# Paired rests transposed into the fourth turned tile's PSUM bank, with an earlier low-rank load and three reorderings in a hybrid attention block

## The chip, the cores and the metric

The kernel runs on one core of a Trainium2 chip. The metric is the device time of one execution in microseconds (us). Five engines take part: TensorE (PE: matmuls and transposes, and PEld, its weight loads), VectorE (DVE), ScalarE (ACT), GpSimd (POOL), and the queues that issue transfers, SyncE (SP) above all. Each engine works through its own instructions in order and waits on semaphores for the others. PE writes only into PSUM, which has eight banks of 128 partitions by 512 float32 values here, and DVE and ACT read the results from there.

## The reference

One encoder layer with two token mixers that read the same normalised input of 512 tokens by 2048 features.

```python
h = rms_norm(x) * (1 + scale) + shift
proj = h @ w_in                       # 2048 -> 7200 columns
aq, ak, av, ag, gq, gk, gv, gg, lr_f, lr_b = split(proj)

# 16 heads x 64, three dilated windows, merged by their softmax denominators
outs, lses = zip(*[dilated_window_attention(aq, ak, av, rel_bias, w, d)
                   for w, d in ((128, 1), (512, 4), (2048, 16))])
att = sum(softmax(lses)[p] * outs[p] for p in range(3))
a_out = att * silu(ag)

# 4 heads, dk 128, dv 256, forward and backward scan
log_g = log_sigmoid(lr @ gate_up + gate_bias) / 16
g_out = rms_norm(gla(q, k, v, log_g_f) + flip(gla(flip(...)))) * gain * silu(gg)

y = concat([a_out, g_out]) @ w_out
out = rms_norm(x + gate * y) * final_gain
```

## The kernel before

**Tiling.** Every large product is done in three matmuls (`three`, L228 to L232): high part by high part, high by low, low by high, with the operands split into two float32r halves. One such matmul is 128 x 128 weights by 512 columns. A *unit* is a 2048 x 512 block of projection columns: `unit` (L1159) runs over 8 groups of weights, 4 output tiles and 2 inner steps, 64 ticks of three matmuls each, and puts the list of side work that it is given between the ticks. Each item of that list has a place between 0 and 1, the share of the 64 ticks after which it is recorded; items at the same place keep the list's order, and items at 1 or more spill into the next unit. PE's order is the order of recording. The orders of DVE, ACT, POOL and SP come from a scheduler that sees the recorded dependences and priorities.

**The order of units.** Start (`sta`, `stb`), then `qk2`, `qk4`, `qk6`, `gk`, each with the attention of four heads beside it (some 200 to 444 us of the span), then the values of the linear attention (`values_unit`, with `gla_head(0)` beside it), `ag0`, `ag1`, `gg0` (each with one more `gla_head`), `gg1`, and the output products `P1`, `P7`, `P6`, `P4`, `P5`, `P3`, `P2` for two pairs of column blocks.

**PSUM.** Two rings: `pj` with five banks (`PJ`), four of which hold a unit's outputs, and `pa` with three (`PA`), through which the side work goes. 

**One head of attention.** A head has four query tiles. `score` (L829) makes a tile's logits (two matmuls into a `pa` bank), DVE adds the bias and takes the minimum (L847), ACT takes the exponent (L851), DVE the reciprocal (L854), POOL scales (L864). The last columns of tiles 1 to 3 are scaled into free columns of tile 0, so that four small *rests* share one 128 x 128 block. Two items later `turn` (L868) transposes three 128 x 128 blocks of the tile on PE (L882) into a `pa` bank `t`; ACT copies them into the high operand `pth` (L888) and DVE takes the low operand `ptl` (L889). When the fourth tile is turned (`i == 3`), `rest` (L896) first transposes the block of rests (L899) into a `pj` bank of its own, `r`, and its four quarters of 32 x 128 are copied and split: for the first two quarters ACT (L906, twice), then DVE (L908, twice), then the same for the other two. `values` (L910) is the head's product with the values (L915, L917), which reads `pth` and `ptl`. The heads below are counted from 0 to 15.

**The low-rank weights.** After unit `gk`, 256 KB of weights are loaded into `lrb` (L1303, SP) and split into `lrs` by ACT (L1306) and DVE (L1307); `low_rank` (L1310) uses them within the values.

**A head of linear attention.** `gla_head` (L1012) returns ten steps: `gates` of the two directions, `turn` of the two (PE transposes `kt`, L1062, ACT copies `kit`, L1064), `states` of the two (PE `kv`, L1074; DVE L1081 and L1086; POOL L1084; ACT L1091), `att` (L1101), two `outs` (L1123), `norm`. `GLA_FIRST` holds the places of head 0 and `GLA_AT` those of the others.

**Before the output products.** `to_s1(1)` and `to_s2(1)` (L1471, L1474: DVE, 128 x 1024 each) form sums for the products `P6` and `P5`. They stand behind the eviction of `gg1` (L1202). A step given to `later(pair, product, group, go)` is recorded when that group's weights are split.

Of the kernel before, what the change touches and what calls it, by code (L numbers as in the profile page):

```python
# [18 lines left out]
P = 128  # L19
S = 512  # L20
D = 2048
KT = D // P
# [95 lines left out]
REST_OF = (14, 11, 2, 15)  # L118
TOKENS = [slice(256 * c + a, 256 * c + 256, 2) for a in range(2) for c in range(2)]

GLA_AT = (0.01, 0.02, 0.33, 0.46, 0.46, 0.56, 0.64, 0.76, 0.76, 0.88)
GLA_FIRST = (0.3, 0.38, 0.55, 0.62, 0.775, 0.81, 0.86, 0.9, 0.92, 0.97)

SUMS_IN = {"ag0": 8, "ag1": 8, "gg0": 8}

# [66 lines left out]
def block_kernel(ctx: ExitStack, tc: tile.TileContext, a: dict):  # L192
# [15 lines left out]
    def T2(name, dt=F32, parts=P):  # L208
        return t2.tile([parts, 512], dt, tag="t2", name=name)
# [4 lines left out]
    def PJ(name):  # L214
        return pp.tile([P, 512], F32, tag="pj", bufs=5, name=name)

    def PA(name):
        return pp.tile([P, 512], F32, tag="pa", bufs=3, name=name)
# [599 lines left out]
    def attention(pairs):  # L818
# [49 lines left out]
        def turn(h, i):  # L868
            def go():
                if not pts:  # L870
                    for z in "hl":
                        pts.append(B8(f"pt{z}", [16, P], F32R))
                        for at, to in ((2, 3), (11, 12)) + ((14, 16),) * (z == "h"):
                            nc.gpsimd.memset(pts[-1][:, at:to, :].bitcast(F32), 0.0)
                if i == 3:
                    rest(h)
                t = pr_.pop((h, i)) if i else pr_[h, i]
                pk = PA(f"t{h}{i}")
                first_ = 0 if i % 2 else 128
                for n_, (c, _) in enumerate(FULL[i]):  # L880
                    kt = (c - i - 1) % 4
                    nc.tensor.transpose(pk[:, n_ * P:n_ * P + P], t[:, first_ + kt * P:first_ + kt * P + P], ident)  # L882
                at, step = FULL[i][0][1], FULL[i][1][1] - FULL[i][0][1]
                hi, lo = (pt[:, at:at + 2 * step + 1:step, :] for pt in pts)
                src = pk[:, :3 * P].rearrange("p (k q) -> p k q", k=3)

                def parts():
                    act(hi, src, AF.Copy)  # L888
                    tt(lo, src, hi.bitcast(F32), op=ALU.subtract)  # L889
                if i or h == heads[0]:  # L890
                    parts()
                else:
                    held_parts.append(parts)
            return go

        def rest(h):  # L896

            pk = PJ(f"r{h}")
            nc.tensor.transpose(pk[:, :P], pr_.pop((h, 0))[:, 0:128], ident)  # L899
            hi, lo = pts  # L900
            to = [(hi, 0, hi, 32), (hi, 0, lo, 0), (hi, 96, lo, 96), (hi, 64, hi, 96)]
            parts = [(t[a:a + 32, REST_OF[i], :], u[b:b + 32, REST_OF[i], :], pk[96 - 32 * i:128 - 32 * i, :P])
                     for i, (t, a, u, b) in enumerate(to)]
            for pair in (parts[:2], parts[2:]):
                for up, _, of in pair:
                    act(up, of, AF.Copy)  # L906
                for up, low_, of in pair:
                    tt(low_, of, up.bitcast(F32), op=ALU.subtract)  # L908
# [103 lines left out]
    def gla_head(h):  # L1012
# [4 lines left out]
        def gates(d):  # L1017
            def go():
                n = f"{h}{d}"
                bias = gbias[:, 4 * d + h:4 * d + h + 1]  # L1020
                pz = PA("z" + n)
                mm(pz, gla["up"][:, d, h * P:h * P + P], gla["lr"], start=True, stop=True)
                e = T2("e" + n)
                act(e, pz, AF.Abs, bias=bias)
                act(e, e, AF.Exp, scale=-1.0)
                act(e, e, AF.Ln, bias=1.0)
                g = T2("g" + n)
                nc.vector.tensor_scalar(g, pz, bias, 0.0, op0=ALU.add, op1=ALU.min)  # L1028
# [12 lines left out]
                act(sc[:, 0, :], b3[:, :, im], AF.Exp, scale=1.0 / 16)  # L1041
                act(sc[:, 1, :], b3[:, :, il], AF.Exp, scale=1.0 / 16)
                bm = T2("bm" + n)
                bm3 = bm.rearrange("p (n t) -> p n t", n=4)
                tt(bm3, b3, b3[:, :, im:im + 1].to_broadcast([P, 4, P]), op=ALU.subtract)
                act(sc[:, 2, :], bm3[:, :, il], AF.Exp, scale=1.0 / 16)
                qi = T2("qi" + n)
                ki = T2("ki" + n)
                act(ki, bm, AF.Exp, scale=-1.0 / 16)
                act(qi, bm, AF.Exp, scale=1.0 / 16)  # L1050
                gq, gk = gla["q"][:, h, :], gla["k"][:, h, :]
                tt(ki, ki, gk, op=ALU.mult)
                tt(qi, qi, gq, op=ALU.mult)
                dirs[d].update(qi=qi, ki=ki, sc=sc, order=[0, 1, 2] if d == 0 else [3, 2, 1])
            return go

        def turn(d):
            def go():
                n, x = f"{h}{d}", dirs[d]
                pk = PA("kt" + n)  # L1060
                for j, c in enumerate(x["order"]):
                    nc.tensor.transpose(pk[:, j * P:j * P + P], x["ki"][:, c * P:c * P + P], ident)  # L1062
                x["kit"] = T2("kit" + n)
                act(x["kit"][:, :384], pk[:, :384], AF.Copy)  # L1064
            return go
# [65 lines left out]
        def norm():  # L1131
# [10 lines left out]
            for v in range(2):  # L1142
                m = 2 * h + v
                if m % 4 == 0:
# [2 lines left out]
                    op0=ALU.mult, op1=ALU.mult)  # L1147

        at = GLA_AT if h else GLA_FIRST
        return list(zip(at, [gates(0), gates(1), turn(0), turn(1), states(0), states(1), att,  # L1150
                             outs(0), outs(1), norm]))

    def urgent(go):
# [137 lines left out]
        for q in range(2):  # L1291
            qk_evict(p + 2 + q, ps[2 * q], ps[2 * q + 1])

    ps = unit("gk", False, attention((6, 7)))
    kp_.close()
    gs = mid.enter_context(tc.tile_pool(name="gs", bufs=1, reuse_waits="tile"))
    gla["k"] = B8("gkt", [4, 512])
# [1 line left out]
        act(gla["k"][:, i, :], ps[i], AF.Copy)  # L1299


    lrb = T2("lrb")
    nc.sync.dma_start(lrb.rearrange("p (k c) -> p k c", k=KT), a["w_lr"][0])  # L1303
    lrs = gp.tile([P, KT, 2, 32], F32R, tag="g", name="lrs")
    lrb3 = lrb.rearrange("p (k c) -> p k c", k=KT)
    act(lrs[:, :, 0, :], lrb3, AF.Copy)  # L1306
    tt(lrs[:, :, 1, :], lrb3, lrs[:, :, 0, :].bitcast(F32), op=ALU.subtract)  # L1307
    plr = PA("plr")
# [172 lines left out]
            (0.65, lambda: to_s1(0)), (0.8, lambda: to_s2(0))]  # L1481
    ps = unit("gg1", False, side + some_sums("gg1"))
    gate_evict(ps, cat[3], "g1")
    to_s1(1)
    to_s2(1)
    mid.close()
    op = ctx.enter_context(tc.tile_pool(name="op", bufs=1, reuse_waits="tile"))
    for e in "hl":
# [184 lines left out]
    for z in range(2):  # L1673
        later(0, "P4", 1 + 2 * z, lambda z=z: halves("A12", z, part(2 + z, 0))())
    later(0, "P1", 1, gate_row)
    later(0, "P4", 2, gain_rows(0))
    later(0, "P4", 3, x_again(0))
    later(1, "P7", 0, x_again(1))
# [129 lines left out]
```

## Time and profile before

| | before |
|---|---|
| time, median of 3 runs | 905.07 us (904.97 to 905.77) |
| profiled execution: time / span | 907.22 us / 905.4 us |
| granted TensorE clock, mean | 0.996 |
| PE busy | 890.0 us, 98% |
| DVE busy | 731.2 us, 81% |
| ACT busy | 491.6 us, 54% |
| POOL busy | 125.9 us, 14% |
| stretch of the attention, 200 to 444 us: PE / DVE / ACT busy | 241.78 / 210.54 / 146.46 of 244 us |

The span runs from the first to the last instruction of the profiled execution, whose own time is 1.8 us longer. Busy times are sums over an engine's instructions; those of different engines overlap. PE's matmuls are pipelined, so that a steady stream starts one every 0.23 us although each is shown as some 0.39 us long; a wait of PE is seen best as a step between two starts that is longer than that.

### The profile page before, as it was taken

The page shows a single profiled execution, that of the slowest core. Times are in us where ns is not written, and L with a number is a line of the kernel's source. Part 1 is how long each engine was busy: PE and PEld are TensorE (multiplying, and loading weights), DVE is VectorE, ACT ScalarE, POOL GpSimd, SP SyncE. Part 2 cuts the span into 40 slices and gives each one's busy share as a digit, 9 for nine tenths or more (in the row PEclk, how much of TensorE's full clock was granted, in tenths as well). Part 3 has the DMA queues.
Part 4 walks back from the last instruction along what each step waited for, and adds up shares of the span by engine and source line. Part 5 has one row for each costly group of instructions (what it writes and reads, how often), then busy time and mean ns, then how long its engine had stood idle before and what let it go on. Part 6 is the DMA issues. An engine that isn't in the chain of part 4 may idle for free.

```text
span 905.4 us, 12339 instructions
## 1 busy us (share of the span) xinstructions
PE 890.0 (98%) x4159; PEld 739.2 (82%) x4159; DVE 731.2 (81%) x1220; ACT 491.6 (54%) x841; POOL 125.9 (14%) x219
## 2 busy tenths in 40 slices
PE   8999999999999999999999999999999999999996
PEld 6888788888888888887778888888888888888885
DVE  7998799878989989888568668595787559797687
ACT  5554533466655745655657554373664248455454
POOL 0000000023323333243000101112020100000001
PEclk9999999999999999999999999999999999999999
DMA  9999489398798898998778879778796988777863
GB/s 342 401 411 363 186 344 367 134 306 226 202 266 273 247 265 247 249 298 223 232 260 255 311 206 308 206 249 262 231 279 208 275 286 289 282 288 249 289 238 154
DMA packets 65547, 242.33 MB, mean 268 GB/s; under 512 B 9190, under 2 KB 11526, under 8 KB 55883
## 3 DMA queue, kind: packets, MB, share of 16 engines
q1 hardware_dynamic: 58724, 199.23, 61.5%
q0 software_dynamic: 6464, 42.01, 19.4%
q8 instruction: 33, 0.54, 0.2%
q10 hardware_dynamic: 296, 0.30, 0.1%
q14 instruction: 30, 0.25, 0.1%
HBM read 224.64 MB, written 51.47 MB: 305 GB/s over the span
## 4 chain that ended last, share of the span: by engine, by line
PE 91%; DVE 3%; ACT 2%; DMA 2%; issue 1%; SPq 0%; DVEq 0%; ACTq 0%
PE ps_qk L230 5%; PE ps_qk L232 5%; PE ps_qk L231 5%; PE g L232 4%; PE g L230 4%; PE g L231 4%; PE stb L232 3%; PE stb L231 3%; PE stb L230 3%; PE ps_ag L232 3%; PE ps_ag L230 3%; PE ps_ag L231 3%; PE o L915 3%; PE sta L230 3%; PE sta L231 3%; PE sta L232 3%
## 5 line engine op out<-in xcount | busy, mean ns | idle before, releaser
L864 POOL TENSOR_SCALAR p<-p,st 128x32 f32<-128x32 f32 (+2 forms) x108 | 59.8, 565 | 159.9 <-DVE st L854 91.2
L328 DVE CUSTOM_DVE_ANT_0 cb<-cb,sb,c_bcond 128x2048 f32<-128x2048 f32 (+1 forms) x32 | 73.4, 2295 | 1.9 <-DMA cb<-in_wm 1.6
L851 ACT ACTIVATE p<-p,st 128x416 f32<-128x416 f32 x64 | 41.0, 641 | 49.2 <-DVE st L847 42.3
L429 POOL DMA_DIRECT2D T<-in_w_o x32 | 23.2, 725 | 159.4 <-ACT V2h L493 14.8
L888 ACT ACTIVATE pth<-t 128x384 fp32r<-128x384 f32 x64 | 31.0, 485 | 19.8 <-PE t L882 11.1
L889 DVE TENSOR_TENSOR ptl<-t,pth 128x384 fp32r<-128x384 f32 x64 | 35.2, 551 | 5.2 <-ACT pth L888 3.7
L882 PE MATMUL t<-c_ident,p 128*128 128x128 f32 x192 | 31.3, 272 | 0.0
L882 PEld LDWEIGHTS t<-c_ident,p 128*128 128x128 f32 x192 | 24.3, 139 | 7.9
L847 DVE CUSTOM_DVE_ANT_0 p<-s,g,st 128x256 f32<-128x256 f32 x64 | 27.7, 432 | 1.8
L847 DVE CUSTOM_DVE_ANT_0 p<-s,g 128x160 f32<-128x160 f32 x64 | 23.5, 367 | 4.2 <-PE s L840 3.5
L328 DVE CUSTOM_DVE_ANT_0 rawg<-rawg,crow,gate 128x1024 f32<-128x1024 f32 x16 | 20.4, 1279 | 4.0 <-DMA rawg<-in_wg 4.0
L1581 POOL TENSOR_SCALAR x<-x,rn 128x512 f32<-128x512 f32 x2 | 2.3, 1167 | 148.5 <-ACT rn L1570 148.5
L429 POOL DMA_DIRECT2D T3V<-in_w_gv x8 | 5.5, 687 | 125.1 <-ACT qk21h L493 118.7
L839 PE MATMUL s<-ks,qh 128*128 128x416 f32 x64 | 22.6, 353 | 0.0
L906 ACT ACTIVATE pth<-r 32x128 fp32r<-32x128 f32 x64 | 17.2, 269 | 9.9 <-PE r L899 4.5
L840 PE MATMUL s<-ks,ql 128*128 128x416 f32 x64 | 22.4, 350 | 0.0
L1091 ACT ACTIVATE sq<-st,sc 128x256 f32<-128x256 f32 x24 | 12.2, 506 | 18.6 <-DVE st L1081 10.0
L328 DVE CUSTOM_DVE_ANT_0 rawg<-rawg,crow,c_bcond 128x1024 f32<-128x1024 f32 x16 | 20.3, 1279 | 0.5 <-DVE g L1028 0.5
L429 POOL DMA_DIRECT2D T<-T x16 | 9.1, 571 | 79.9 <-ACT V8h L493 12.9
L915 PE MATMUL o<-pth,vv 128*128 128x512 f32 (+1 forms) x64 | 15.9, 369 | 2.2 <-DVE pth L908 1.1
L466 DVE TENSOR_TENSOR raw_O<-raw_O,raw_P 128x1024 f32<-128x1024 f32 x8 | 9.8, 1225 | 10.1 <-DMA raw_O<-in_w_o 7.8
L568 ACT ACTIVATE h_hi<-xt,shift 128x512 fp32r<-128x512 f32 x16 | 11.5, 721 | 10.3 <-DVE shift L328 9.5
(1661 smaller groups left out, 3151.6 us busy)
## 6 DMA issues: line engine op xcount, KB each, us to landing
cb<-in_wm SPq DMA_DIRECT2D x31, 1024.0 KB, 9.3
T<-in_w_o POOLq DMA_DIRECT2D x32, 512.0 KB, 6.5
rawg<-in_wg SPq DMA_DIRECT2D x32, 512.0 KB, 5.4
raw_O<-in_w_o SPq DMA_DIRECT2D x32, 512.0 KB, 4.6
raw_qk<-in_w_qk SPq DMA_DIRECT2D x24, 512.0 KB, 4.9
raw_O<-T SPq DMA_DIRECT2D x24, 512.0 KB, 5.0
rawb<-in_w_sb SPq DMA_DIRECT2D x16, 512.0 KB, 8.9
rawv<-in_wv SPq DMA_DIRECT2D x16, 512.0 KB, 5.6
```

Of the source, the lines that this page charges most:

```text
L230: mm(ps, lh, rh, start=first, stop=False, skip_group_check=more)
L231: mm(ps, ll, rh, start=False, stop=False, skip_group_check=more)
L232: mm(ps, lh, rl, start=False, stop=last, skip_group_check=more)
L328: return nc.vector.tensor_tensor_reduce(out=w, in0=w, in1=with_, op0=ALU.mult, op1=ALU.add, scale=1.0, scalar=init, accum_out=dst)
L429: move = nc.gpsimd.dma_start(dst, src, max_dma_last_dim=8192, **how).ins
L847: top = nc.vector.tensor_tensor_reduce(out=t[:, lo:hi], in0=ps[:, lo:hi], in1=gt[h][:, at:at + 2 * (hi - lo) - 1:2], op0=ALU.add, op1=ALU.min,
L851: act(t, t, AF.Exp, bias=st[:, 0:1], scale=-1.0, accum_out=st[:, 1:2])
L864: last["pool"] = nc.gpsimd.tensor_scalar(to, of, st[:, 2:3], 1.0, op0=ALU.mult, op1=ALU.mult).ins
L882: nc.tensor.transpose(pk[:, n_ * P:n_ * P + P], t[:, first_ + kt * P:first_ + kt * P + P], ident)
L888: act(hi, src, AF.Copy)
L889: tt(lo, src, hi.bitcast(F32), op=ALU.subtract)
L915: mm(po[:, P * a0:P * a1], vv[h // 4][:, c, h % 4, :], pt[:, at:at + (a1 - a0 - 1) * step + 1:step, :], start=n_ == z == 0, stop=False, sk ...
```

## The change

The rests' transpose no longer takes a bank of its own. `turn` takes its `pa` bank `t` first and hands `rest` the last quarter of it, columns 384 to 511; the three transposes of the fourth tile, which are recorded behind `rest`, write columns 0 to 383 of the same bank. Line numbers behind L892 fall by one or rise by a few. The load of `lrb` becomes an item at 0.7 of unit `gk`. In the linear attention the first direction's states come ahead of the second direction's turn for heads 1 to 3 (with the second turn at 0.47 in place of 0.46); for head 0 the places are swapped with the list, so that only its two `outs` move, from 0.9 and 0.92 to 0.91 and 0.93. `to_s1(1)` and `to_s2(1)` are recorded in group 1 of the first `P1`.

```diff
-GLA_AT = (0.01, 0.02, 0.33, 0.46, 0.46, 0.56, 0.64, 0.76, 0.76, 0.88)
-GLA_FIRST = (0.3, 0.38, 0.55, 0.62, 0.775, 0.81, 0.86, 0.9, 0.92, 0.97)
+GLA_AT = (0.01, 0.02, 0.33, 0.46, 0.47, 0.56, 0.64, 0.76, 0.76, 0.88)
+GLA_FIRST = (0.3, 0.38, 0.55, 0.775, 0.62, 0.81, 0.86, 0.91, 0.93, 0.97)
...
+                pk = PA(f"t{h}{i}")
                 if i == 3:
-                    rest(h)
+                    rest(h, pk[:, 3 * P:])
                 t = pr_.pop((h, i)) if i else pr_[h, i]
-                pk = PA(f"t{h}{i}")
...
-        def rest(h):
-
-            pk = PJ(f"r{h}")
-            nc.tensor.transpose(pk[:, :P], pr_.pop((h, 0))[:, 0:128], ident)
+        def rest(h, pk):
+
+            nc.tensor.transpose(pk, pr_.pop((h, 0))[:, 0:128], ident)
             hi, lo = pts
             to = [(hi, 0, hi, 32), (hi, 0, lo, 0), (hi, 96, lo, 96), (hi, 64, hi, 96)]
-            parts = [(t[a:a + 32, REST_OF[i], :], u[b:b + 32, REST_OF[i], :], pk[96 - 32 * i:128 - 32 * i, :P])
+            parts = [(t[a:a + 32, REST_OF[i], :], u[b:b + 32, REST_OF[i], :], pk[96 - 32 * i:128 - 32 * i, :])
                      for i, (t, a, u, b) in enumerate(to)]
...
-        return list(zip(at, [gates(0), gates(1), turn(0), turn(1), states(0), states(1), att,
+        return list(zip(at, [gates(0), gates(1), turn(0), states(0), turn(1), states(1), att,
                              outs(0), outs(1), norm]))
...
-    ps = unit("gk", False, attention((6, 7)))
+    lrb = []
+
+    def lr_load():
+        lrb.append(T2("lrb"))
+        nc.sync.dma_start(lrb[0].rearrange("p (k c) -> p k c", k=KT), a["w_lr"][0])
+
+    ps = unit("gk", False, attention((6, 7)) + [(0.7, lr_load)])
...
-    lrb = T2("lrb")
-    nc.sync.dma_start(lrb.rearrange("p (k c) -> p k c", k=KT), a["w_lr"][0])
...
-    to_s1(1)
-    to_s2(1)
...
+    later(0, "P1", 1, lambda: (to_s1(1), to_s2(1)))
```

The first place is PE where head 4's rests and fourth tile are transposed, in unit `qk4` (`ps_qk` its outputs, `p` the scaled tiles, `c_ident` the identity; in brackets the engines whose semaphores an instruction waits for). Before:

```order
L232 MATMUL ps_qk_0_2253<-h_lo,qk43h 128x512
L899 MATMUL r_2487<-c_ident,p_2324 128x128 [waits Pool_49]
L882 MATMUL t_2497<-c_ident,p_2409 128x128 [waits DVE_49,PE_49,Activation_49]
L882 MATMUL t_2497<-c_ident,p_2409 128x128 x2
L230 MATMUL ps_qk_1_2254<-h_hi,qk43h 128x512
L231 MATMUL ps_qk_1_2254<-h_hi,qk43l 128x512
L232 MATMUL ps_qk_1_2254<-h_lo,qk43h 128x512
```

The same place on PE after the change:

```order
L232 MATMUL ps_qk_0_2249<-h_lo,qk43h 128x512
L898 MATMUL t_2483<-c_ident,p_2320 128x128 [waits DVE_49,PE_49,Pool_49]
L882 MATMUL t_2483<-c_ident,p_2405 128x128 [waits DVE_49,Activation_49]
L882 MATMUL t_2483<-c_ident,p_2405 128x128 x2
L230 MATMUL ps_qk_1_2250<-h_hi,qk43h 128x512
L231 MATMUL ps_qk_1_2250<-h_hi,qk43l 128x512
L232 MATMUL ps_qk_1_2250<-h_lo,qk43h 128x512
```

All four transposes now write one tile, `t_2483`. The first of the three has a wait for DVE of its own, and in the built program the value that this wait asks for is the one that the fourth and last of head 4's L907 brings; this holds for each of the 16 heads. Before, head 4's wait for DVE asked for the L847 that had last read the bank.

The second place is DVE at the same head, where the low parts of the rests are taken (L908 before, L907 after; `rawv` is a bias sum beside the attention, `s` the next tile's logits). Before:

```order
L998 ISA rawv_2329,vbias_1498<-rawv_2329,shb 128x1024 [waits DMAHW6_49,DMAHW4_49]
L998 ISA vbias_1498 128x1
L854 RECIPROCAL st_2467<-st_2467 128x1 [waits Activation_49]
L908 TENSOR_TENSOR pth<-r_2487,pth 32x128 [waits PE_49]
L908 TENSOR_TENSOR ptl<-r_2487,pth 32x128
L847 ISA p_2509,st_2510<-s_2506,g_2341 128x160 [waits PE_49,Pool_49]
L847 ISA st_2510 128x1
L889 TENSOR_TENSOR ptl<-t_2497,pth 128x3x128
L847 ISA p_2509,st_2510<-s_2506,g_2341,st_2510 128x256 [waits DVE_49]
L847 ISA st_2510 128x1
L908 TENSOR_TENSOR ptl<-r_2487,pth 32x128 [waits Activation_49]
L1249 TENSOR_TENSOR S_2514<-S_2414,h_hi 128x512 [waits Pool_49]
```

The same place on DVE after the change:

```order
L997 ISA rawv_2325,vbias_1498<-rawv_2325,shb 128x1024 [waits DMAHW6_49,DMAHW4_49]
L997 ISA vbias_1498 128x1
L854 RECIPROCAL st_2463<-st_2463 128x1 [waits Activation_49]
L907 TENSOR_TENSOR pth<-t_2483,pth 32x128 [waits PE_49]
L907 TENSOR_TENSOR ptl<-t_2483,pth 32x128
L907 TENSOR_TENSOR ptl<-t_2483,pth 32x128 [waits Activation_49]
L907 TENSOR_TENSOR pth<-t_2483,pth 32x128
L889 TENSOR_TENSOR ptl<-t_2483,pth 128x3x128 [waits Activation_49]
L847 ISA p_2504,st_2505<-s_2501,g_2337 128x160 [waits PE_49,Pool_49]
```

The four low parts now stand together, ahead of the fourth tile's own low part (L889) and of the next logits; between the second and the third DVE waits for ACT. What stands ahead of the first is as it was.

The third place is PE in unit `gg0`, where head 3 of the linear attention turns its keys for the second direction (`kt`) and its states begin (`kv`). Before:

```order
L1062 MATMUL kt_6219<-c_ident,ki_6092 128x128 [waits DVE_49]
L1062 MATMUL kt_6219<-c_ident,ki_6092 128x128 x2
L1074 MATMUL kv_6225<-gv_5001,kit_6183 128x256 [waits Activation_49]
L1074 MATMUL kv_6225<-gv_5001,kit_6183 128x256
L1074 MATMUL kv_6226<-gv_5001,kit_6183 128x256 [waits PE_49]
L230 MATMUL ps_gg_3_6034<-h_hi,gg03h 128x512
```

The same place on PE after the change:

```order
L1073 MATMUL kv_6203<-gv_4985,kit_6167 128x256 [waits Activation_49]
L1073 MATMUL kv_6203<-gv_4985,kit_6167 128x256
L1073 MATMUL kv_6204<-gv_4985,kit_6167 128x256 [waits DVE_49]
L230 MATMUL ps_gg_3_6018<-h_hi,gg03h 128x512
L231 MATMUL ps_gg_3_6018<-h_hi,gg03l 128x512
L232 MATMUL ps_gg_3_6018<-h_lo,gg03h 128x512
L1061 MATMUL kt_6227<-c_ident,ki_6076 128x128 [waits DVE_49,PE_49]
L1061 MATMUL kt_6227<-c_ident,ki_6076 128x128 x2
```

The three `kv` of the first direction now come first, and the turn of the second direction follows one tick of three matmuls later.

More of the change, by code (lines that the diff above doesn't have):

```diff
@@ L1299, in block_kernel @@
         act(gla["k"][:, i, :], ps[i], AF.Copy)
-    lrb = T2("lrb")
-    nc.sync.dma_start(lrb.rearrange("p (k c) -> p k c", k=KT), a["w_lr"][0])
     lrs = gp.tile([P, KT, 2, 32], F32R, tag="g", name="lrs")
-    lrb3 = lrb.rearrange("p (k c) -> p k c", k=KT)
+    lrb3 = lrb[0].rearrange("p (k c) -> p k c", k=KT)
     act(lrs[:, :, 0, :], lrb3, AF.Copy)
```

## The prediction

> **What bounds the kernel now.** I read the page first, then PE's waits, then the timeline at the places that the change touches.
>
> ```profile
> span 905.4 us, 12339 instructions
> PE 890.0 (98%) x4159; PEld 739.2 (82%) x4159; DVE 731.2 (81%) x1220; ACT 491.6 (54%) x841; POOL 125.9 (14%) x219
> PE 91%; DVE 3%; ACT 2%; DMA 2%; issue 1%; SPq 0%; DVEq 0%; ACTq 0%
> ```
>
> PE is busy for 98% of the span and holds 91% of the chain that ended last: a microsecond that PE stands still is a microsecond of the end, and work on other engines costs nothing until PE waits for it. So I look for where PE waits now, and where it will wait. The view of PE's waits (engine, line, what it waited for; us in total, times, longest) has little:
>
> ```profile
> PE sta L591 <- ACT h_hi L534: 2.7, 1, 2.7
> ...
> PE o L915 <- DVE pth L908: 1.1, 1, 1.1
> PE o L915 <- ACT pth L888: 1.0, 1, 1.0
> PE go L1123 <- ACT V27h L493: 0.3, 1, 0.3
> ```
>
> The first stands at the start and is not touched. The two `o` waits are the most that the first two edits could remove:
>
> ```profile
> 416.82 0.40 PE L232 MATMUL ps_gk<-h_lo,gk5h 128*128 128x512 f32 x1
> 418.32 0.47 PE L915 MATMUL o<-pth,vv 128*128 128x512 f32 x1 [1.10 <-DVE pth L908]
> ...
> 440.92 0.39 PE L232 MATMUL ps_gv_P<-V0l,h_hi 128*128 128x512 f32 x1
> 442.31 1.13 PE L915 MATMUL o<-pth,vv 128*128 128x512 f32 x4 [1.01 <-ACT pth L888]
> ```
>
> A matmul of this kind starts 0.23 us after the one before it (two rows 0.23 apart, below). So PE lost 418.32 − 416.82 − 0.23 = 1.27 us and 442.31 − 440.92 − 0.23 = 1.16 us, 2.4 us together.
>
> **The rests in t's bank: what it removes and what it adds.** It removes no instruction; the same 16 + 192 transposes and 64 + 64 small evictions run. It removes the bank `r`. But `rest` is recorded ahead of the three transposes of the fourth tile, and they now write the bank that the rests are read from. In the built order the first of them waits for the last of the four L907 on DVE. That is a new wait on PE, once for each of 16 heads, and everything on PE stands behind it: PE works in order, and the unit's matmuls that used to cover the evictions come after it. Here is what happened there before, at head 4, in the timeline of all engines:
>
> ```profile
> 271.62 0.39 PE L232 MATMUL ps_qk<-h_lo,qk43h 128*128 128x512 f32 x1
> 271.85 0.27 PE L899 MATMUL r<-c_ident,p 128*128 128x128 f32 x1
> 271.95 0.49 PE L882 MATMUL t<-c_ident,p 128*128 128x128 f32 x3
> 272.15 0.56 ACT L906 ACTIVATE pth<-r 32x128 fp32r<-32x128 f32 x2 [0.65 <-PE r L899]
> ...
> 272.99 1.22 DVE L998 CUSTOM_DVE_ANT_0 rawv<-rawv,shb 128x1024 f32<-128x1024 f32 x1
> ...
> 274.32 0.30 DVE L908 TENSOR_TENSOR pth<-r,pth 32x128 fp32r<-32x128 f32 x1
> ...
> 274.63 0.28 DVE L908 TENSOR_TENSOR ptl<-r,pth 32x128 fp32r<-32x128 f32 x1
> ...
> 274.95 0.56 ACT L906 ACTIVATE pth<-r 32x128 fp32r<-32x128 f32 x2 [1.11 <-DVE ptl L908]
> ...
> 276.18 0.29 DVE L908 TENSOR_TENSOR ptl<-r,pth 32x128 fp32r<-32x128 f32 x1
> ...
> 277.19 0.28 DVE L908 TENSOR_TENSOR pth<-r,pth 32x128 fp32r<-32x128 f32 x1
> ```
>
> Before, the three transposes start 0.10 us behind the rests', whatever the evictions do; the last of these ends 277.47 − 271.85 = 5.6 us later, hidden. The row at 274.95 shows that the evictions are a chain: ACT stood idle for 1.11 us until DVE's second one, though the two read other partitions of the bank. Two engines take turns at one bank, a pair at a time. So the chain is PE, ACT pair, DVE pair, ACT pair, DVE pair, and PE's next transposes have now become its fifth link.
>
> *Its least length*, with ACT and DVE free: 0.27 (the transpose) + 0.56 + 0.59 + 0.56 + 0.59 (pairs, from the rows: 274.91 − 274.32 for DVE's) + 5 hand-overs of 0.03 to 0.04 (272.15 − 272.12, 274.95 − 274.91) = 2.7 us, less the 0.10 us that PE spends there anyway: 2.6 us. *Its length with the lag that DVE has now*: in the built order nothing is taken from ahead of the first L907, but the second pairs now follow at once in most heads. For head 4 the first DVE pair ended 274.91 − 271.85 = 3.06 us behind the rests' transpose, because DVE had a bias sum of 1.22 us ahead of it. The other end, head 9:
>
> ```profile
> 348.78 0.27 PE L899 MATMUL r<-c_ident,p 128*128 128x128 f32 x1
> ...
> 350.15 0.28 DVE L908 TENSOR_TENSOR ptl<-r,pth 32x128 fp32r<-32x128 f32 x1
> ```
>
> 1.65 us, with nothing in the way. Read in the same way, the 16 heads lie at 1.65 to 3.06 us, mean 2.3. Adding a second ACT pair and DVE pair with their hand-overs, 1.25 us, and taking off 0.10, the wait is 2.8 to 4.2 us, mean 3.5. While PE stands, DVE (busy for 210.54 of the 244 us of the attention) loses its backlog, which pulls the mean towards 2.6, but what stands ahead of the pair is mostly paced by PE itself and stays. I take 3.3, nearer to the rows with the lag: 16 x 3.3 = **52.8 us**, with ends of 42 (2.6 each) and 60 (3.75 each, some longer where L847 or a split stands between the pairs). Nothing covers it: the only PE work that could is behind the wait.
>
> **The clock after such a gap.** PE would now stand still some 16 times for about 3 us. What a gap does to the granted clock, this trace shows at its two ends (the columns: stretch, us, busy time of PE, PEld, DVE, ACT, POOL; PEclk; DMA):
>
> ```profile
> 7.87:11.28 3.41, 1.03 (x5) 0.84 (x6) 2.81 (x6) 2.23 (x5) 0.00 (x0) 1.00 1.03 407
> 11.28:14.69 3.41, 3.41 (x10) 2.64 (x9) 2.31 (x3) 1.00 (x2) 0.00 (x0) 0.50 1.03 429
> ...
> 895.33:898.74 3.41, 1.59 (x7) 0.97 (x6) 2.31 (x6) 2.23 (x6) 0.99 (x1) 1.00 0.26 102
> 898.74:902.16 3.42, 0.00 (x0) 0.00 (x0) 2.10 (x5) 2.01 (x6) 0.00 (x0) 1.00 0.77 309
> 902.16:905.40 3.24, 0.00 (x0) 0.00 (x0) 0.00 (x0) 0.00 (x0) 0.00 (x0) 0.50 0.54 214
> ```
>
> The clock changes at steps of 3.41 us. A stretch in which PE was idle for 2.38 of 3.41 us was followed by one at half clock; one with 1.82 us idle was not. Gaps that fall anywhere on these steps and leave PE idle for 3.1 us put at least 2.38 us into one stretch in (0.31 + 2 x 0.72) / 3.41 = 51% of the cases, and at least 1.82 us in 84%; I take the middle, 68%, 11 heads. Half a stretch is lost each time, 1.7 us, less what the gap itself still takes of it: 1.6 us. That is 11 x 1.6 = **17 us**, with ends of 0 and 26.
>
> [...]
>
> **The other edits.** *The load of `lrb`.* Now ACT stands before it and holds the head's `pth` (L888) for the wait at 442.31:
>
> ```profile
> 441.12 0.63 ACT L1306 ACTIVATE lrs<-lrb 128x512 fp32r<-128x512 f32 x1 [2.78 <-DMA lrb<-in_w_lr]
> lrb<-in_w_lr SPq DMA_DIRECT2D x1, 256.0 KB, 6.6
> ```
>
> The load goes ahead of 512 KB of weights, and ACT and DVE meet `lrs` within head 14, some 15 us earlier. Those queued behind it are the exponent and the second half of the logits of head 15's first tile, and behind these PE's turn. If the load still takes 6.6 us it lands up to 2 us after ACT asks for it. Between 0 and +2 us; I take 0, since head 14's own new gap lies just behind and takes the wait in.
>
> With both edits the 2.4 us of the two `o` waits go: behind the gaps the evictions are done before PE gets to `o`. Nothing else is late there.
>
> *The reorderings.* PE's other steps that are too long are 0.3 to 0.45 us each: before `go` (row above), before `kt` in `gg0`, and before O2's low half, where DVE had `to_s1(1)` first:
>
> ```profile
> 525.13 0.46 PE L1123 MATMUL go<-at,gv 128*128 128x128 f32 x2 [0.28 <-ACT V27h L493]
> ...
> 667.38 0.55 PE L1062 MATMUL kt<-c_ident,ki 128*128 128x128 f32 x3
> ...
> 673.16 1.46 PE L1074 MATMUL kv<-gv,kit 128*128 128x256 f32 x6
> ...
> 674.17 0.48 DVE L1086 SCALAR_TENSOR_TENSOR st<-kv,sc,dc 128x256 f32<-128x256 f32 x1 [0.38 <-POOL dc L1084]
> ```
>
> At most −1 us. Against it: with the turn behind the first states, `kv` of the second direction reuses the first direction's banks, and in head 3 its third matmul, at about 673.6, must wait for the L1086 that ends at 674.65: +1 us. I take −0.5 together, with ends of −1 and +1.5.
>
> **The sum.** 52.8 + 17 − 2.4 − 0.5 = +67 us. Against the profiled execution, 907.2 us (span 905.4 and 1.8 around it), that is 974; the median of the three runs is 2.15 below that execution, 905.07, and gives 972. I say **970 us**, the gaps' backlog being likelier smaller than larger.
>
> **Rivals.** *(1) The gaps without the half clock.* For it: a gap is shorter than a step of the clock, and the one case at the start comes just after warming up. Against it: the row with PEclk 0.50. It gives 905.07 + 52.8 − 2.9 = 955 us. *(2) Longer gaps and the half clock nearly every time.* Where exponents or a unit's evictions stand between the two pairs, as now in half of the heads: 905.07 + 60 + 16 x 1.65 − 3 = 989 us. *(3) Faster: no turn at the bank on PE.* If the wait that stands in the built order were met when PE arrives, only the gains would be left: 905.07 − 2.4 − 1 = 901.6 us. It decides at the point where the last L907 ends no later than 0.10 us behind the rests' transpose; head 9's second eviction alone, half of the chain, ended 1.65 us behind, the shortest of the 16, and that speaks against it in every head. It is also the case in which the change does what its words say.
>
> [...] The row at 274.95 shows turns by the whole bank, and the sum goes by it.
>
> **How the numbers follow.** Forecast 0.70, with its own range of 953 to 987 (42 + 14 − 3 to 60 + 24 − 2); rival 1 0.16; rival 2 0.09; rival 3 0.05. Two in ten left out on both sides make 946 to 988. A measurement tells some 0.2% (1.8 us) from no change: faster 0.04, same 0.01 (rival 3 with its gains given back), slower 0.95.
>
> **What would show it.** In the profile after: PE's waits list `t` L882 <- DVE `pth` L907, 16 times, with 2.4 to 4 us each and some 50 us in all; no `o` L914 wait; a mean granted clock below 0.996, near 0.98, and half-clock stretches between 208 and 445 us; the stretch of the attention longer by 60 to 70 us and every later stage of the same length. PE's busy time says little, since matmuls at half clock count as longer. I am wrong if the L882 rows follow L898 within 0.2 us, if the clock stays full (then near 955), or if the gaps are below 2.5 us.

## The result, and the profile after

The changed kernel takes 991.22 us (median of 6 runs, 990.17 to 993.25) against 905.66 us before (904.97 to 906.37): 1.0947 times the time, with an interval of 1.0933 to 1.0961. The prediction said 970 us and a range of 946 to 988; the time lies 3 us above that range. Its mechanism is there, and larger than it said.

From the page of the profile after: the span, the engines' busy time, and the chain that ended last.

```profile
span 988.4 us, 12347 instructions
PE 919.3 (93%) x4159; PEld 759.6 (77%) x4159; DVE 733.7 (74%) x1220; ACT 493.8 (50%) x841; POOL 120.3 (12%) x219
...
PE 81%; DVE 9%; ACT 5%; DMA 3%; issue 2%; POOL 0%; SPq 0%; DVEq 0%; ACTq 0%; POOLq 0%
```

The same instructions of DVE and ACT take the same time as before (733.7 and 731.2, 493.8 and 491.6 us), but 9% and 5% of the chain now run through them. PE, the engine that set the end, waits for them. The view of PE's waits after (engine, line, what it waited for; us in total, times, longest) says where:

```profile
PE t L882 <- DVE pth L907: 55.1, 16, 4.2
PE kv L1073 <- ACT kit L1063: 2.6, 1, 2.6
...
PE sta L591 <- ACT h_hi L534: 1.1, 2, 0.9
```

The first row is the predicted one, once for each of 16 heads. The two `o` waits and the `go` wait are gone. The second row is new and was not in the prediction. Here is head 4 after, the head that the prediction showed before, in the timeline (start, duration, engine, line, operation, tiles; in brackets the idle time before it and what ended it):

```profile
292.64 0.39 PE L232 MATMUL ps_qk<-h_lo,qk43h 128*128 128x512 f32 x1
292.87 0.27 PE L898 MATMUL t<-c_ident,p 128*128 128x128 f32 x1
293.17 0.56 ACT L905 ACTIVATE pth<-t 32x128 fp32r<-32x128 f32 x2 [0.65 <-PE t L898]
...
294.01 1.22 DVE L997 CUSTOM_DVE_ANT_0 rawv<-rawv,shb 128x1024 f32<-128x1024 f32 x1
...
295.34 0.29 DVE L907 TENSOR_TENSOR pth<-t,pth 32x128 fp32r<-32x128 f32 x1
295.65 0.28 DVE L907 TENSOR_TENSOR ptl<-t,pth 32x128 fp32r<-32x128 f32 x1
295.97 0.55 ACT L905 ACTIVATE pth<-t 32x128 fp32r<-32x128 f32 x2 [1.11 <-DVE ptl L907]
...
296.85 0.28 DVE L907 TENSOR_TENSOR pth<-t,pth 32x128 fp32r<-32x128 f32 x1
297.28 0.74 PE L882 MATMUL t<-c_ident,p 128*128 128x128 f32 x3 [4.14 <-DVE pth L907]
297.67 0.78 PE L230 MATMUL ps_qk<-h_hi,qk43h 128*128 128x512 f32 x1
298.25 0.63 PE L231 MATMUL ps_qk<-h_hi,qk43l 128*128 128x512 f32 x1
298.67 0.63 PE L232 MATMUL ps_qk<-h_lo,qk43h 128*128 128x512 f32 x1
```

Read it from the top: PE, ACT, DVE, ACT, DVE, PE, with the bias sum of 1.22 us still ahead of DVE's first pair. PE's step from the rests' transpose to the next is 297.28 − 292.87 = 4.41 us instead of 0.11. The last three rows show the second cost: behind the gap a matmul that took 0.39 us takes 0.63, and the next one starts 0.42 us later in place of 0.23.

Means over the 16 heads, in us behind the start of the rests' transpose:

| | first ACT pair | first DVE pair | second ACT pair | second DVE pair | PE's next transpose |
|---|---|---|---|---|---|
| before | 0.58 to 1.14 | 1.56 to 2.33 | 2.90 to 3.46 | 3.75 to 4.74 | 0.11 |
| after | 0.51 to 1.08 | 1.51 to 2.28 | 2.35 to 2.91 | 2.99 to 3.57 | 3.71 |

The second pairs follow at once now, as predicted. The first DVE pair ends 2.28 us behind in place of 2.33: DVE is as late as it was. And PE starts 0.14 us behind DVE's last eviction, where 0.03 to 0.04 was assumed. ACT's second pair again waits for DVE's first (the row at 295.97, 1.11 us), so the turns go by the whole bank, as the prediction took them; whether a wait of each eviction for its own 32 partitions alone would shorten the chain was not tried.

The clock: the view of stretches after, at steps of 3.41 us (stretch, us, busy time of PE, PEld, DVE, ACT, POOL; PEclk; DMA).

```profile
225.76:229.18 3.42, 1.31 (x7) 0.78 (x5) 2.08 (x8) 1.81 (x6) 1.35 (x4) 1.00 0.59 192
229.18:232.59 3.41, 2.67 (x9) 2.37 (x10) 1.13 (x3) 0.97 (x2) 0.00 (x0) 0.50 0.12 43
232.59:236.00 3.41, 3.41 (x11) 2.72 (x10) 2.64 (x7) 1.31 (x3) 0.26 (x1) 0.50 0.00 0
430.56:433.98 3.42, 1.56 (x9) 0.99 (x7) 2.97 (x7) 3.01 (x7) 0.13 (x1) 1.00 1.13 344
433.98:437.39 3.41, 1.70 (x9) 1.51 (x10) 2.05 (x5) 1.41 (x4) 0.00 (x0) 1.00 0.91 208
```

In the first group PE is busy for 1.31 of 3.42 us; the next step runs at half clock. That step begins with the tail of the gap (PE busy 2.67 of 3.41 us), and the one behind it is at half clock *again*, although PE now never stands still. In the second group another gap, of 3.7 us, falls astride two steps, 1.56 and 1.70 us busy, and nothing happens. In the whole attention 14 of the 16 gaps are followed by a half-clock step and five of these by a second one: 19 steps, 64.9 us. PE's order in the attention is the same before and after, so that its starts can be compared one by one: at these steps they lie 27.2 us further apart than before, 1.4 us for each step. (The expectations below take 24.8 us for it, which is too little.)

### The profile page after: what moved, and what is told of

It is laid out like the page before. It is cut to its first block, busy times and chain, and to the rows that moved or that the text cites. A ratio compares the mean times of both kernels' runs of the same rounds, so it can differ in the third digit from the quotient of the medians.

```text
span 988.4 us, 12347 instructions
## 1 busy us (share of the span) xinstructions
PE 919.3 (93%) x4159; PEld 759.6 (77%) x4159; DVE 733.7 (74%) x1220; ACT 493.8 (50%) x841; POOL 120.3 (12%) x219
## 4 chain that ended last, share of the span: by engine, by line
PE 81%; DVE 9%; ACT 5%; DMA 3%; issue 2%; POOL 0%; SPq 0%; DVEq 0%; ACTq 0%; POOLq 0%
PE ps_qk L230 4%; PE ps_qk L231 4%; PE ps_qk L232 4%; PE g L232 4%; PE g L230 3%; PE g L231 3%; PE stb L232 3%; PE stb L231 3%; PE stb L230 3%; PE ps_ag L230 3%; PE ps_ag L232 3%; PE ps_ag L231 3%; PE ps_gv_P L231 3%; PE ps_gv_P L230 3%; PE ps_gv_P L232 3%; PE o L914 2%
## 5 line engine op out<-in xcount | busy, mean ns | idle before, releaser
L882 PE MATMUL t<-c_ident,p 128*128 128x128 f32 x192 | 35.9, 301 | 55.1 <-DVE pth L907 55.1
L851 ACT ACTIVATE p<-p,st 128x416 f32<-128x416 f32 x64 | 41.1, 642 | 84.7 <-DVE st L847 77.4
L864 POOL TENSOR_SCALAR p<-p,st 128x32 f32<-128x32 f32 (+2 forms) x108 | 54.0, 509 | 238.6 <-DVE st L854 125.8
L889 DVE TENSOR_TENSOR ptl<-t,pth 128x384 fp32r<-128x384 f32 x64 | 35.4, 553 | 31.9 <-ACT pth L888 29.7
L888 ACT ACTIVATE pth<-t 128x384 fp32r<-128x384 f32 x64 | 30.9, 483 | 40.9 <-PE t L882 40.8
L847 DVE CUSTOM_DVE_ANT_0 p<-s,g 128x160 f32<-128x160 f32 x64 | 23.7, 370 | 33.4 <-PE s L840 31.4
L847 DVE CUSTOM_DVE_ANT_0 p<-s,g,st 128x256 f32<-128x256 f32 x64 | 27.7, 434 | 2.1
L905 ACT ACTIVATE pth<-t 32x128 fp32r<-32x128 f32 x64 | 17.1, 268 | 16.6 <-DVE ptl L907 10.8
L1122 PE MATMUL go<-qi,sq 128*128 128x128 f32 x96 | 15.9, 275 | 0.0
L840 PEld LDWEIGHTS s<-ks,ql 128*128 128x128 f32 x64 | 13.4, 209 | 3.3
```

Source lines behind the costliest of these rows:

```text
L840: mm(ps[:, :NK], ql[:, q], ks[:, k], start=False, stop=True)
L847: top = nc.vector.tensor_tensor_reduce(out=t[:, lo:hi], in0=ps[:, lo:hi], in1=gt[h][:, at:at + 2 * (hi - lo) - 1:2], op0=ALU.add, op1=ALU.min,
L851: act(t, t, AF.Exp, bias=st[:, 0:1], scale=-1.0, accum_out=st[:, 1:2])
L864: last["pool"] = nc.gpsimd.tensor_scalar(to, of, st[:, 2:3], 1.0, op0=ALU.mult, op1=ALU.mult).ins
```

## Experiments

Each kernel ran beside the kernel before on the same chip (905.6 to 905.9 us there).

### The rests undone, and the rests alone

Two halves of the change: the changed kernel with `rest` writing a `pj` bank of its own again, and the kernel before with only the rests' edit.

```diff
-                    rest(h, pk[:, 3 * P:])
+                    rest(h)
...
-            nc.tensor.transpose(pk, pr_.pop((h, 0))[:, 0:128], ident)
+            pk = PJ(f"r{h}")
+            nc.tensor.transpose(pk[:, :P], pr_.pop((h, 0))[:, 0:128], ident)
```

> The changed kernel with the rests back in a pj bank of their own; the load and the three reorderings stay. Theory (PE's turn behind the rests' evictions, and the half clock that these gaps bring, are nearly the whole loss): no wait of PE at the fourth tile's transposes, no half-clock stretch in the attention, and about 906.8 us (905 to 908.5): 905.7 of before, plus the 2.7 us wait of the keys' product in the last head of linear attention, less 1.2 and 0.4 for two waits that go. Rival (load or reorderings carry a large part of the loss): above 915 us.

> The kernel before with the rests' edit alone. Theory: 16 gaps of 3.6 us in front of the fourth tile's transposes (57.6 us), some 19 half-clock steps that cost 24.8 us, less 2.4 us of waits for the head's product: 905.7 + 80 = 985.7 us (982 to 989), and no wait of the keys' product in linear attention. Rival (the edits make each other worse): below 975 us.

Measured: the rests undone 907.17 us (ratio 1.0022, 1.0008 to 1.0037); the rests alone 985.59 us (1.089, 1.0873 to 1.0907). Both lie within half a microsecond of the theory. PE's waits with the rests undone:

```profile
PE kv L1074 <- ACT kit L1064: 2.6, 1, 2.6
...
PE o L915 <- DVE pth L908: 1.1, 1, 1.1
```

and with the rests alone:

```profile
PE t L882 <- DVE pth L907: 54.2, 16, 4.2
```

So the rests' edit is nearly the whole loss, and the other edits together cost 1.4 us. The two parts do not quite add: 79.9 and 1.4 make 81.3 of the 85.6 us. One part of the rest, 0.8 us, can be read: with the load moved as well, the split of `lrb` on DVE (0.69 us) stands ahead of head 14's chain, and the gaps of heads 14 and 15 are 4.35 and 3.00 us against 3.91 and 2.62 with the rests alone. The remaining 3.5 us are not settled, and two candidates can be named. One is the `o` wait on L888 (1.2 us), which the gaps remove with or without the earlier load. The other is half-clock steps: counted as above, they cost 27.2 us in the profile after and 25.6 us in that of the rests alone. Between the medians it may be more, since the other five executions of the changed kernel have a lower granted clock than the profiled one (0.961 to 0.963 against 0.965).

### Work for PE in the gap: is it the idle time that halves the clock?

```diff
                     rest(h, pk[:, 3 * P:])
+                    keep = PJ(f"keep{h}")
+                    for _ in range(12):
+                        mm(keep, h_hi[:, 0, :P], h_hi[:, 0, :], start=True, stop=True)
```

> The changed kernel with 12 matmuls of 128 x 512 recorded between the rests' transpose and the fourth tile's three; their result, in a bank of its own, is read by nobody. They add 16 x 12 x 0.227 = 43.6 us of PE work, all inside the gaps. Theory (the half clock comes of PE standing idle, and a step of 3.41 us needs about 2 us of idle time for it): the step from the rests' transpose to the next stays at 3.7 us on average, of which about 1 us is idle; no half-clock step in the attention; 991.2 - 24.8 = 966.4 us (962 to 971), faster with more work. Rival (the half clock has another cause than PE's idle time): 19 half-clock steps as now and 986 us or more.

Measured: 966.19 us (964.01 to 970.91), 25.0 us faster than the changed kernel with 192 matmuls more. The four executions lie in two pairs: 964.0 and 964.1 us at a granted clock of 0.998, which is 27 us faster, and 968.3 and 970.9 us at 0.994 and 0.992. The profile is of the slowest. The step from the rests' transpose to the fourth tile's three stayed (3.75 us on average). The stretches of this kernel:

```profile
287.27:290.68 3.41, 2.04 (x12) 1.54 (x11) 1.47 (x5) 1.02 (x3) 0.74 (x2) 1.00 0.92 324
475.00:478.42 3.42, 0.97 (x5) 0.46 (x3) 2.75 (x11) 1.27 (x4) 1.16 (x2) 1.00 0.81 274
478.42:481.83 3.41, 2.88 (x9) 2.40 (x10) 1.02 (x3) 0.49 (x1) 1.63 (x4) 0.50 0.94 278
481.83:485.24 3.41, 3.41 (x19) 2.92 (x18) 0.99 (x5) 1.32 (x4) 0.00 (x0) 1.00 0.71 130
```

The first row is the longest of the usual gaps: 2.04 us busy, and no half clock follows. Of the heads only 14 has a half-clock step in this execution, where DVE was late and the chain took 6.0 us, longer than twelve matmuls cover. Two more such steps come behind the attention, with PE at work: at 731.00 us, from the wait of `kv`, and at 853.88 us, from a wait of 2.1 us for DVE's L477 that the changed kernel's profile doesn't have. So the half clock comes of PE's idle time, and costs 25 to 27 us here. The median close to the 966.4 us of the theory is in part luck, with a term that was too small and half-clock steps that it didn't foresee. The other 60 us of the loss are mostly the gaps, and the wait of `kv`.

> The changed kernel with 4 idle matmuls in each gap in place of 12: 0.9 us of 3.6 filled, 2.1 to 3.4 us left idle. If a step of 3.41 us needs 1.85 to 2.04 us of PE idle time to be followed by a half-clock one (the ends that the 16 heads of the changed kernel showed), a gap of this size falls astride two steps in some 6 of 16 cases and escapes: 10 half-clock runs of steps, 981 us (977 to 986). Rival (any wait of PE of more than 2 us halves the clock, wherever it falls): 14 of 16 as now, 988 us or more. Rival (only a step idle from end to end counts): none, 966 us.

Measured, with `range(4)`: 978.1 us (975.68 to 984.66), and in the profiled execution exactly 10 heads with one half-clock step each, so that neither rival holds. The time is 3 us below the middle that the theory gave; no gap had a second step here. Three stretches lie close to the points at which the clock falls or comes back; each is shown with the stretch behind it. Two are of this kernel:

```profile
501.98:505.39 3.41, 1.52 (x9) 1.23 (x9) 1.59 (x6) 1.28 (x5) 0.00 (x0) 1.00 0.62 247
505.39:508.81 3.42, 3.42 (x10) 2.67 (x9) 0.26 (x1) 1.70 (x3) 0.00 (x0) 0.50 0.00 0
...
406.40:409.81 3.41, 2.73 (x8) 2.34 (x9) 1.13 (x3) 0.50 (x2) 0.55 (x2) 0.50 0.86 284
409.81:413.22 3.41, 3.41 (x18) 2.86 (x18) 1.59 (x6) 0.84 (x3) 0.46 (x1) 1.00 0.02 7
```

and one is of the kernel of the next experiment, behind which the clock stayed full:

```profile
470.18:473.60 3.42, 1.51 (x8) 0.93 (x6) 2.62 (x10) 1.81 (x6) 1.29 (x4) 1.00 0.46 151
473.60:477.01 3.41, 2.51 (x15) 2.22 (x16) 2.02 (x7) 1.55 (x2) 0.53 (x1) 1.00 0.86 205
```

In the profiles before and after, steps at full clock with 1.56 us of PE or more were followed by full clock, those with 1.38 us or less by half clock. Three lie between: 1.52 (the first row) and 1.54 (the kernel `rests_last` below) went down, 1.51 did not. So in these profiles the point lies at about 1.5 us of 3.41. On the way back it is another: at half clock 2.67 us busy was not enough (after, the step from 229.18 us) and 2.73 was (above), and no step in the profiles before and after says otherwise.

### Four evictions on ACT, then four on DVE

```diff
-            for pair in (parts[:2], parts[2:]):
+            for pair in (parts,):
```

> The changed kernel with the rests' evictions as four on ACT and then four on DVE, in place of two, two, two and two. Theory (the gap is ACT's and DVE's time laid end to end plus the time until DVE is free): DVE's lag now runs beside two more evictions of ACT, and the gap falls from 3.60 to 3.16 us on average, 7 us over 16 heads; with 12 or 13 heads at half clock in place of 14 the time is 982 us (978 to 986). Rival (DVE's lag is only shifted, nothing of it overlaps): 988 us or more.

Measured: 983.57 us (981.79 to 984.64), with gaps of 3.25 us on average and 13 heads at half clock. ACT's four now end 1.65 us behind the rests' transpose, DVE's run from 1.89 to 3.22, PE goes on at 3.36. So DVE's lag does overlap with ACT's second pair, though by 0.35 us rather than 0.44. It also shows what neither order can take away as long as the two engines take turns: four evictions of 0.28 us and four of 0.29, one after the other, are 2.3 us.

### The rests behind the three transposes

The bank stays shared; only the order in it changes. In the first kernel the rests' transpose comes behind the tile's three and their evictions ahead of the tile's own; in the second the tile's own evictions come first.

```diff
-                if i == 3:
-                    rest(h, pk[:, 3 * P:])
                 t = pr_.pop((h, i)) if i else pr_[h, i]
...
                     nc.tensor.transpose(pk[:, n_ * P:n_ * P + P], t[:, first_ + kt * P:first_ + kt * P + P], ident)
+                if i == 3:
+                    rest(h, pk[:, 3 * P:])
```

In the second, that place holds the rests' transpose alone, and the evictions follow the tile's:

```diff
                     parts()
+                    if i == 3:
+                        rest(h, pk[:, 3 * P:])
```

> The changed kernel with the rests still in the fourth tile's bank, but their transpose recorded behind the three of the tile, and their evictions ahead of the tile's. Theory (it is the order inside the bank that makes PE wait, not the sharing): PE's four transposes go in one piece, no wait there, full clock, 904 to 908 us. Rival (sharing the bank costs by itself, since the tile's own evictions come last and the bank is held some 2 us longer, so that the next logits or turns wait for a pa bank): 1 to 3 us at each head, 920 to 955 us.

> As the experiment with the rests' transpose behind the three, but the evictions of the tile itself come first and those of the rests last; the rests still share the bank. Theory (what that experiment lost, 12 us against the kernel with the rests undone, was the tile's own operands arriving behind the rests' four turns, just ahead of the head's product): the tile's operands are early again and the rests end about a microsecond later than with a bank of their own: 908 to 913 us, waits of PE for the head's product of 4 us in all at most. Rival (the bank held longer is what costs, whichever evictions come last): 917 to 921 us as there.

Measured: evictions of the rests first 919.08 us (918.48 to 920.09), evictions of the tile first 911.17 us (910.5 to 914.95). The wait for L907 is gone in both, and with it 72 and 80 us. So the gap came of the order inside the bank. The first missed its forecast of 904 to 908: one end of a chain was forgotten. Its timeline at head 4, where the product reads what the tile's own eviction writes:

```profile
304.10 1.06 ACT L493 ACTIVATE qk61h<-raw_qk 128x1024 fp32r<-128x1024 f32 x1 [0.34 <-PE ps_qk L232]
...
304.54 0.28 DVE L907 TENSOR_TENSOR pth<-t,pth 32x128 fp32r<-32x128 f32 x1
...
305.07 0.47 ACT L888 ACTIVATE pth<-t 128x384 fp32r<-128x384 f32 x1
...
305.59 1.08 PE L914 MATMUL o<-pth,vv 128*128 128x512 f32 x4 [0.46 <-ACT pth L888]
...
307.44 0.90 PE L914 MATMUL o<-ptl,vv 128*128 128x384 f32 x3 [0.59 <-DVE ptl L889]
```

The tile's own copy (L888) comes behind the last of the rests, at this head also behind an eviction for the unit on ACT (L493), and PE's product waits for the copy; `ptl` (L889) is late in the same way on DVE. PE's waits in this kernel:

```profile
PE o L914 <- ACT pth L888: 4.1, 6, 1.6
...
PE o L914 <- DVE ptl L889: 1.5, 3, 0.6
```

The kernel takes 12 us more than with the rests undone. With the tile's evictions first 8 of those 12 us come back, so the order of the evictions made most of it; what is left above the kernel with the rests undone is 4.0 us, of which PE's waits show 1.9 at one logits product and 1.2 at `o`:

```profile
PE s L839 <- DVE ptl L889: 1.9, 1, 1.9
...
PE o L915 <- ACT pth L906: 1.2, 2, 0.6
```

In the profiled execution (913.52 us) the first of these waits also brings a half-clock step, at 428.68 us, behind one in which PE was busy for 1.54 us.

In no order that was tried did the shared bank beat a bank of its own (911.17 us at best against 907.17).

### The linear attention's order, the load and the sums

> The kernel before with the linear attention's reordering alone. Theory: in the last head's pair of directions the copy of the second turned keys stands on ACT behind the three scaled states of the first direction, and the second product of keys and values on PE waits 2.7 us for it; the 0.44 us wait of the head's outputs goes: 905.7 + 2.7 - 0.4 = 908.0 us (906.5 to 909.5). Rival (the wait is covered elsewhere, as the prediction had it): 904.7 to 905.7 us.

> The same, with PE's order unchanged, but for heads 1 to 3 the first direction's states are recorded behind the second direction's turn, so that ACT copies the turned keys ahead of the three scaled states. Theory (ACT's order makes the wait): no wait of the second product, 905.3 us (904 to 906.8). Rival (the product waits for a bank that the first direction's states still read): a wait of 1 to 2.7 us remains, 906.5 to 908 us.

The second of these leaves PE's order as in the first and changes only where the first direction's states are recorded:

```diff
-        return list(zip(at, [gates(0), gates(1), turn(0), states(0), turn(1), states(1), att,
+        return list(zip(at, [gates(0), gates(1), turn(0)] +
+                             ([states(0), turn(1)] if h == 0 else
+                              [products(0), lambda: (turn(1)(), states(0)())]) + [states(1), att,
```

(`products` holds the matmuls of `states`.) Measured: 908.68 us (ratio 1.0032, 1.0017 to 1.0046) and 904.59 us (0.9991, 0.9981 to 1.0001). ACT's order makes the wait. The timeline of the changed kernel at that place:

```profile
749.54 0.49 PE L1061 MATMUL kt<-c_ident,ki 128*128 128x128 f32 x3
...
753.08 0.39 PE L232 MATMUL ps_gg<-h_lo,gg04h 128*128 128x512 f32 x1
...
754.59 0.48 DVE L1085 SCALAR_TENSOR_TENSOR st<-kv,sc,dc 128x256 f32<-128x256 f32 x1 [0.38 <-POOL dc L1083]
755.10 0.51 ACT L1090 ACTIVATE sq<-st,sc 128x256 f32<-128x256 f32 x1 [1.48 <-DVE st L1085]
755.52 0.47 ACT L1063 ACTIVATE kit<-kt 128x384 f32<-128x384 f32 x1
...
756.04 0.70 PE L1073 MATMUL kv<-gv,kit 128*128 128x256 f32 x2 [2.58 <-ACT kit L1063]
```

The keys are turned at 750.03, and ACT has 1.48 us with nothing to do, but its copy of them is queued behind the third scaled state, which waits for DVE, which waits for POOL. In the split order the same copy starts 0.25 us after the turn:

```profile
665.84 0.49 PE L1062 MATMUL kt<-c_ident,ki 128*128 128x128 f32 x3
666.58 0.47 ACT L1064 ACTIVATE kit<-kt 128x384 f32<-128x384 f32 x1
```

This wait, too, can halve the clock. With the rests undone, PE was busy for 0.85 us of the step from 670.83 us, and the next ran at half clock (profiled execution, 910.03 us); with the reordering alone the wait fell astride two steps and none followed (profiled execution, 906.78 us). The seven executions of that kernel take 906.6 to 906.8 us at a granted clock of 0.997, and 908.6 to 910.1 us at 0.993 to 0.995. So the wait seems to cost about 1 us in some executions and 3 us or more in others, which would make the 3.1 us between the medians a mixture; of the slower ones of this kernel there is no trace.

> The kernel before with the earlier load of the low-rank weights and the two sums in the first output product, nothing else. Theory: the 1.16 us wait of the last head's product goes, the sums move nothing: 904.5 us (903.3 to 905.7). Rival (the split of the low-rank weights, now met within head 14, holds up logits and turns there): 906 us or more, with a wait of PE near 430 to 440 us.

> The kernel before with the earlier load, the moved sums and the linear attention in the split order; the rests keep their own bank. Theory: the gains add: 905.6 - 1.0 - 1.1 = 903.5 us (902.3 to 904.8), with one wait of PE for the head's product (1.1 us, on the low part of head 13's rests) left in the attention. Rival (the gains hide each other, since work that PE doesn't wait for only moves): 904.6 us or more.

Measured: 904.95 us for the load and the sums (0.9995, 0.9986 to 1.0005: not told from no change), and 904.36 us for these with the split order (0.9979, 0.9969 to 0.9989), 1.5 us below the kernel before and the lowest median of the study. The `o` wait on L888 is gone in both. That alone doesn't show a gain of the load: the wait is also gone in the profile of the split order alone, and 0.3 us instead of 1.0 in that of the reordering alone, and neither moves the load. With the load and the sums PE also waits once, at 507 us, for DVE's L477 (0.7 us), a wait that no other profile has at this place. One wait inside the attention is left in both:

```profile
PE o L915 <- DVE pth L908: 1.1, 1, 1.1
```

## Why the prediction fell short, and what of it was right

| term | predicted, us | measured, us |
|---|---|---|
| 16 gaps on PE | +52.8 (42 to 60) | +57.6 |
| half clock behind them | +17 (0 to 26) | +27.2 from the starts, 25 to 27 by experiment |
| two `o` waits | −2.4 | −2.4 |
| reorderings | −0.5 (−1 to +1.5) | +2.7 for `kv`, −0.4 for `go` |
| load and split of `lrb` | 0 (0 to +2) | +0.8 within the gaps of heads 14 and 15, counted there |

The measured terms make 84.7 us; the two profiled executions lie 990.17 − 907.22 = 82.95 apart. Some 0.8 us of the difference lie ahead of the attention, where a wait at the start (L591) is shorter in the execution after, and another 0.8 us in small steps at the heads' products (L914). The medians lie 85.56 apart, since the execution after is 1.05 us below its median and that of before 1.56 above its own. The granted clock bears this out: 0.965 in the execution after against 0.961 to 0.963 in the other five, which is one or two half-clock steps more in those (a step of 3.41 us at half clock is 0.0017 of the mean).

**The direction and the mechanism** stand: PE's turn behind four evictions, 16 times, and a half clock behind most. The experiments with the rests undone and with the rests behind the three transposes show the first, those with matmuls in the gaps the second.

**The step that failed most is the size of the clock term** (17 us predicted, 27.2 measured), in two of its factors. First, "I take the middle, 68%, 11 heads": the two stretches that the trace before offers leave the point between 1.82 and 2.38 us idle, and it lies at its low end, about 1.9 (1.51 to 1.54 of 3.41 us busy). The prediction's own formula gives 84% for that end, 13.4 heads; 14 were measured. Second, "Half a stretch is lost each time", 1.6 us: a step cost 1.4 us, but a gap that runs on into the half-clock step keeps the clock down for another whole one, which five heads showed, and so the 14 heads lost 1.9 us each. That a half-clock step needed more work to come back (2.73 us of PE) than a full one to stay up (1.56 us) was in no row of before, and the sum had no room for it.

**The gap** was marked down from 3.5 to 3.3 us because DVE "loses its backlog" while PE stands. DVE's first pair ended 0.05 us earlier, of 2.33: what stands ahead of it, such as the bias sum of head 4, came with PE's progress as before, which the same sentence of the prediction half allowed. The rows said 3.5, the measurement 3.60, and the remaining 0.1 is PE's own hand-over of 0.14 us. The 2 us that were taken off the sum of 972 for a smaller backlog went the wrong way for the same reason.

**The reorderings** were priced by the wrong queue. The prediction looked for a conflict at the bank of `kv` (+1 us in head 3) and didn't read ACT's order at this place, where the copy of the turned keys now stands behind three scaled states. One wait of 2.7 us outweighs all gains of the small edits: with the rests undone they cost 1.4 us.

**The load of `lrb`** behaved as taken: no wait of its own on PE, and a price that hides in head 14's gap, since its split stands ahead of DVE's first pair there. Without the gaps no gain of it is shown: with the sums alone beside it the measured 0.6 us can't be told from none, and the `o` wait that it was to remove differs between kernels that don't move it.

**The range** ended at 988 although the separate upper ends (60, 26, +1.5, −2.4) reach 990: the ends were set as if the costs were independent, but longer gaps brought both more half clock and longer half clock (14 heads and five second steps here, ten and none with four matmuls in the gap). What came is nearest to rival 2 (60 us of gaps and a half clock nearly every time, 989 us), which got a chance of 0.09.

## What to carry to other kernels

Before two PE results share a PSUM bank, look at what is recorded between them: if the first is read before the second is written, PE waits for the whole chain of evictions, here 3.60 us on average in 16 heads, and everything behind it waits too. Put PE's writes to one bank in one piece (919.08 us in place of 991.22), and then check whether the readers that come last are still early enough for what follows (911.17 with the tile's evictions ahead of the rests'). When PE must stand still, ask not only how long, but how much of each step of the clock is left busy: work that nobody reads can be worth its place, as 12 matmuls in each gap showed (25.0 us faster). And when an item is moved for PE's sake, read the order of the engine that evicts it: a ready copy waited on ACT behind one that wasn't, from 750.03 us, where the keys were turned, to 755.52.

## What was not expected of the hardware

The clock fell behind steps of 3.41 us in which PE had been busy for as much as 1.54 us, 45% of the step (`rests_last`), and it came back only behind a step with at least 2.7 us, 80% (2.67 us was not enough in the changed kernel, 2.73 was with four matmuls in the gap). Short gaps were enough: with four matmuls in the gap, what was left of it in heads 12 and 15 was 2.2 and 2.1 us (the step of 3.20 and 3.10 us less 0.11 and the matmuls' 0.91), and both brought a half-clock step, since they fell mostly into one step. Conversely two gaps of 3.0 and 3.7 us, each astride two steps, brought none in the changed kernel.

Nor did a step have to be idle from end to end. The second rival of the experiment with four matmuls took it so, and gave 966 us; measured were 978.1.
